# Down-projection of a transformer block: sums added to the rows by two accumulating DMAs, and a fifteenth Strassen pair in the second half

## The chip, the cores and the metric

One NeuronCore of a Trainium2 chip runs the whole program. The metric is the device time of one execution in microseconds (us). The core has a matrix engine (PE in the profile, with PEld for its weight loads), a vector engine (DVE), a scalar engine (ACT), GpSimd (POOL), a queue engine that issues transfers (SP), and 16 DMA engines that all queues share. Each engine runs its own list of instructions strictly in order, and waits on semaphores of the others.

## The reference

One decoder layer on 256 tokens of width 2048 in float32. The part that matters here is the end of it:

```python
D_FF = ((8 * D_MODEL // 3 + 255) // 256) * 256        # 5632

def conv_glu_ffn(h, w_up, cw, cb, w_down):
    u = causal_depthwise_conv(h @ w_up, cw, cb)
    a, gate = jnp.split(u, 2, axis=-1)
    return (jax.nn.silu(gate) * a) @ w_down
...
    x = x + jnp.concatenate([attn, conv], axis=-1) @ w_out[l]
    h = rms_norm(x, ffn_norm_g[l])
    x = x + conv_glu_ffn(h, w_up[l], ffn_conv_w[l], ffn_conv_b[l], w_down[l])
return rms_norm(x, final_norm_g)
```

The down-projection multiplies the gated rows g (256 x 5632) by w_down (5632 x 2048) and adds the product to the rows x, which are then normed and written out.

## The kernel before, in words

**Halves and pairs.** The down-projection runs in two halves of 1024 output columns (`for h in range(2)`). Each half takes 22 pairs of 128-row slices of w_down. Below the pairs are counted through both halves: 0 to 21 are the first half, 22 to 43 the second. A half holds eight PSUM banks (`nb`): four of them (names 2, 3, 4, 8) collect the four 128 x 512 quarters of the output, the other four (1, 5, 6, 7) collect corrections that Strassen pairs need. The two halves use the eight banks in turned roles (`ring`), so a bank of the second half is free when what the first half left in it has been read.

**Two kinds of pair.** `KINDS` has a letter for each pair. A direct pair (D) is eight products of a 128-row slice. A Strassen pair (S) is seven products, in the order of `products`; the third and fourth use sums of gated slices (`gs`, part 1), the fifth and sixth use sums of gated slices (`gs`, part 0) and sums of weights (`xh`, `xl`). Every product is four matmuls in split precision: a float32 operand is held as a high part and a low part (`wh` and `wl` for weights, `gh` and `gl` for gated slices), so each weight chunk costs ACT one copy (`wh`) and DVE one subtraction (`wl`), line 113 and 114. A Strassen chunk costs more: DVE makes three sums of weights (lines 139 and 142, tile `sums`, one buffer), and ACT and DVE split these into `xh` and `xl`. Tiles `xh` and `xl` share a ring of four buffers (`tag="xt"`), so two Strassen chunks are under way at a time. The subtraction that gives `xl` is written at the start of the next chunk's split (`lows`).

**Order of the work.** The program is written out by hand; nothing reorders it. `down_pair` runs up to four entries of a list `todo` (five before pair 21), then `w_next` splits the chunk two pairs ahead, then the pair's matmuls are issued. Splitting a chunk also lets SP issue the transfer of the chunk four ahead (`w_dma`).

**POOL's queue.** During the down-projection POOL only issues transfers: `gl` (512 KB, the low parts of four gated slices, at every second pair, line 1083) and `gs` (two of 256 KB for each Strassen pair, two pairs ahead, line 1090). Earlier, in the up-projection, POOL also writes the third weight sum of each Strassen chunk into DRAM with one plain and two accumulating transfers of 256 KB (line 1108), and forms the sums of gated slices for all pairs that are S in either half (`SPAIRS`, lines 1099 to 1101).

**Between the halves.** When the last Strassen pair of a half (pair 20) has been issued, `combine` is put on `todo`: ACT copies bank 1 to `cuv`, and eight DVE additions put the corrections into the rows `x2`. `cuv` has the buffer of `sums`, so the next Strassen split waits for it. At pair 22 four `first_add` (DVE: rows plus the four main banks) and four `first_half` (ACT: squares for the final norm; DVE: product with the final gain) follow.

Of the kernel before, what the change touches and what calls it, by code (L numbers as in the profile page):

```python
# [11 lines left out]
F32 = mybir.dt.float32  # L12
F32R = mybir.dt.float32r
AF = mybir.ActivationFunctionType
OP = mybir.AluOpType
PSUM = bass.MemoryType.PSUM

P = 128
# [16 lines left out]
CW = 2048  # L35
# [1 line left out]

SLOT = {(0, 0): 0, (1, 1): 1, (1, 0): 2, (0, 1): 3}
KINDS = ("DDDDSSDSSSSDSSSSDSSSSD",
         "DDSDSSDSSSDSSSSDSSSSDD")  # L40
SPAIRS = [p for p in range(22) if "S" in KINDS[0][p] + KINDS[1][p]]

CUTS = ((0, 1), (1, 2), (2, 4), (4, 5), (5, 6), (6, 8), (8, 10), (10, 12), (12, 14), (14, 16))
# [10 lines left out]
def hybrid_trunk(ctx: ExitStack, tc: tile.TileContext, a: dict, out: bass.AP):  # L54
    nc = tc.nc
# [123 lines left out]
    def w_next(cuts=1, ahead=LA):  # L179
        c = st["use"]  # L180
        st["use"] += 1
        w_pump()
        if st["split"] >= len(chunks):
            for f in lows:
                f()
            lows.clear()
        while st["split"] <= min(c + ahead, len(chunks) - 1):
            w_pump()
            w_split(cuts)
        if cuts == 1 or POOLED[0] <= st["split"] - 1 < POOLED[1]:  # L190
            w_pump()
        now = late[:]
        late.clear()
        if now:
            clock["dve"] = max(clock["dve"], clock["pe"])
        for f in now:
            f()
        return parts.pop(c)
# [54 lines left out]
    mixp = ctx.enter_context(tc.tile_pool(name="mix", bufs=1))  # L253
    xt = [mixp.tile([P, 4, 2, T], F32R, name="xt", bufs=4) for _ in range(4)]
# [3 lines left out]
    with ExitStack() as mx:  # L258
# [60 lines left out]
        for n, ((lo, hi), (xc, *wc)) in enumerate(zip(CUTS, heads)):  # L319
            xs = [(xc[:, (k - lo) * T:(k - lo + 1) * T], k) for k in range(lo, hi)]  # L320
            sl = slice(lo * P, hi * P)
            if n < EARLY:
                h, l = parts[0]
# [291 lines left out]
        for n in range(4):  # L615
            kv, i = divmod(n, 2)
# [360 lines left out]
        x2 = None  # L977
# [31 lines left out]
        for n, (qr, g) in enumerate(OUT_ORDER):  # L1009
# [3 lines left out]
            if n == 2:  # L1013
                x2 = mixp.tile([P, 2, D], F32, name="x2")
# [40 lines left out]
    with ExitStack() as fx:  # L1055
# [49 lines left out]
        for c in sorted(c for c in kinds if kinds[c] == "S"):  # L1105
            src, far = chunks[c][0], spill.tile([P, 512], F32, name=f"sum{c - down0}")
# [109 lines left out]
        names = {(0, 0): 2, (0, 1): 3, (1, 0): 4, (1, 1): 8}  # L1216
# [9 lines left out]
        def run_todo(n):  # L1226
            for _ in range(min(n, len(todo))):
                todo.pop(0)()

        def down_pair(h, p, g, j, nb):  # L1230

            kind = KINDS[h][p]
            if j == 0 and h + p:
                g_load()
            run_todo(5 if 22 * h + p == 21 else 4)
            if not late_pool:
                ws = w_next()
                while stages:
                    up_stages()
                up_only.close()  # L1240
                late_pool.append(fx.enter_context(tc.tile_pool(name="fd", bufs=1)))
                sum_load(22 * h + p + 2, 1)
            else:
                sum_load(22 * h + p + 2, 1)
                ws = w_next()
            sum_load(22 * h + p + 2, 0)
            if kind == "S":
                gsum = sq.pop(0)
            for name, gi, w in products(kind, j):
                left[h, name] -= 1  # L1250
                wh, wl = [v[:, w % 4 * 512:(w % 4 + 1) * 512] for v in ws[w // 4 * 2:][:2]]
                xh, xl = [v[:, gi] for v in g] if gi < 8 else [gsum[gi // 2 % 2][:, i, gi % 2] for i in range(2)]
                mm_down(nb[name], xh, xl, wh, wl, (h, name) not in begun, left[h, name] == 0)
                begun.add((h, name))

        def combine(h, nb):

            x = {k: x2[:, k[0], h * 1024 + k[1] * 512:h * 1024 + (k[1] + 1) * 512] for k in names}
            s = {}

            def alloc():
                t = late_pool[0].tile([P, 1536], F32, name="cuv", tag="sums", bufs=1)
                s.update({n: t[:, i * 512:(i + 1) * 512] for i, n in enumerate("cuv")})
                nc.scalar.activation(s["c"], nb[1], AF.Copy)

            add, sub = nc.vector.tensor_add, nc.vector.tensor_sub
            return [alloc, lambda: add(x[0, 1], nb[5], x[0, 1]), lambda: add(x[1, 1], nb[5], x[1, 1]),
                    lambda: add(s["u"], nb[6], s["c"]), lambda: sub(s["v"], s["u"], nb[7]),
                    lambda: add(x[0, 0], x[0, 0], s["c"]), lambda: sub(x[0, 1], x[0, 1], s["u"]),
                    lambda: add(x[1, 0], x[1, 0], s["v"]), lambda: sub(x[1, 1], x[1, 1], s["v"])]  # L1270

        def first_add(nb, t, n):
            xq = x2[:, t, n * 512:(n + 1) * 512]
            nc.vector.tensor_add(xq, nb[names[t, n]], xq)

        def first_half(t, n):
            xq = x2[:, t, n * 512:(n + 1) * 512]
            nc.scalar.activation(sq3[:, :512], xq, AF.Square, accum_out=ss3[:, t, n:n + 1])
            nc.vector.tensor_mul(xq, xq, gfin[:, n * 512:(n + 1) * 512])
# [3 lines left out]
        def last_rows(w0, w1_, g, b0, t):  # L1283
            for i, (lo, hi) in enumerate(LAST):
                b = (b0, bank[2 + t], bank[4 + t])[i][:, :hi - lo]
                for j, ws in enumerate((w0, w1_)):
                    for k in range(2):
                        n = lo // 512
                        c = slice(SLOT[k, n] * 512 + lo - n * 512, SLOT[k, n] * 512 + hi - n * 512)
                        gs = 4 * j + 2 * k + 1 - t  # L1290
                        mm_down(b, g[0][:, gs], g[1][:, gs], ws[0][:, c], ws[1][:, c],
                                i > 0 and j + k == 0, j + k == 2)
                xq = x2[:, t, 1024 + lo:1024 + hi]
                if i == 2:
                    acc = mean_of(fw, [ss3[:, t, i:i + 1] for i in range(3)], D)
                nc.vector.tensor_add(xq, b, xq)
                nc.scalar.activation(sq3[:, :hi - lo], xq, AF.Square, accum_out=ss3[:, t, 2 + i:3 + i])
            r3 = rstd_of(fw, [ss3[:, t, i:i + 1] for i in range(3, 5)], D, acc)
            xq = x2[:, t].rearrange("p (a b c) -> p a b c", a=2, b=2)
            for i in range(2):  # L1300
                nc.scalar.activation(xq[:, 0, i], xq[:, 0, i], AF.Copy, scale=r3)
                nc.vector.scalar_tensor_tensor(xq[:, 1, i], xq[:, 1, i], r3, gfin[:, 1024 + i * 512:1536 + i * 512],
                                               op0=OP.mult, op1=OP.mult)
                nc.sync.dma_start(out_rows[:, t].rearrange("p (a b c) -> p a b c", a=2, b=2)[:, :, i], xq[:, :, i])

        begun, todo, left = set(), [], {}
# [5 lines left out]
                for name in (2, 4):  # L1312
                    left[h, name] += 1
        ring = bank[2:] + bank[:2]
        prev = None
        for h in range(2):
            nb = dict(zip((2, 3, 4, 8, 1, 5, 6, 7), ring[4 * h:] + ring[:4 * h]))
            for q in range(NQ):
                g = gq.pop(0)
                if h == 1 and q == NQ - 1:  # L1320
                    run_todo(99)
                    for t in range(2):
                        nc.vector.tensor_add(x2[:, t, 1536:], nb[names[t, 1]], x2[:, t, 1536:])
                    w0 = w_next()
                    w1_ = w_next()
                    for t in range(2):
                        last_rows(w0, w1_, g, nb[names[t, 0]], t)
                    break
                if prev and q == 0:
                    todo.extend(lambda t=t, n=n, nb=prev: first_add(nb, t, n) for t in range(2) for n in range(2))  # L1330
                    todo.extend(lambda i=i: first_half(i // 2, i % 2) for i in range(4))
                for j in range(2):
                    p = 2 * q + j
                    down_pair(h, p, g, j, nb)
                    if KINDS[h].rfind("S") == p:
                        todo.extend(combine(h, nb))
            prev = nb


def _buckets():  # L1340
# [87 lines left out]
```

## Time and profile before

| what | value |
|---|---|
| median of 3 runs | 1086.2 us (1086.03 to 1087.13) |
| the profiled execution, its time | 1086.44 us |
| its span on the core | 1084.7 us |
| up-projection on PE | to 849.2 us |
| down-projection on PE | 849.2 to 1075.2 us |
| granted PE clock | 1.00 in all stretches read here |

Times of rows are counted from the start of the span. The span is 1.74 us shorter than the execution. In an answer on stretches of time, each engine's busy time is followed by its number of instructions, then come the granted PE clock, the mean busy share of the 16 DMA engines and what they moved in GB/s. In a timeline row stand the start, the duration, the engine, the line, the operation, out<-in and the count; what the engine waited for just before is in brackets. A row on transfers has the size and the median time from issue to landing; a row on a queue (q0 is POOL's, q1 is SP's) has its packets, MB and share of the engines' time in that stretch.

### The profile page before, as it was taken

What the parts mean: (1) busy time and instruction counts of PE and PEld (TensorE: products, weight loads), DVE (VectorE), ACT (ScalarE), POOL (GpSimd) and SP (SyncE); (2) the same over time, 40 slices, a digit from 0 to 9 for tenths busy, and PEclk for the clock granted to TensorE, in tenths of its full rate; (3) what the DMA queues carried; (4) which work ended last, traced back from release to release, by engine and by line L of the source; (5) the groups of instructions that cost most, each with busy time, mean ns of one, the idle gap of its engine ahead of it and who ended that gap; (6) DMA issues with size and microseconds to landing.
All of it is one profiled execution on the core that took longest, in us unless ns stands there. A gap on an engine that the chain in (4) does not pass through costs nothing.

```text
span 1084.7 us, 17486 instructions
## 1 busy us (share of the span) xinstructions
PE 1073.1 (99%) x6730; PEld 956.5 (88%) x6730; DVE 878.1 (81%) x1399; ACT 615.7 (57%) x892; POOL 360.4 (33%) x411
## 2 busy tenths in 40 slices
PE   9999999999999999999999999999999999999996
PEld 9999999998788888888888888888888888888885
DVE  7899975777456677778787888878787899999996
ACT  7544366778635555556555555556555555655563
POOL 0888856657100202324233433212121222211220
PEclk9999999999999999999999999999999999999998
DMA  9676536323464788999999999966667699979882
GB/s 353 244 262 241 187 99 231 121 79 117 177 225 168 241 267 255 284 289 270 299 279 308 277 300 296 283 222 224 223 222 279 214 390 344 350 283 356 320 315 80
DMA packets 60048, 270.46 MB, mean 249 GB/s; under 512 B 7947, under 2 KB 10779, under 8 KB 39868
## 3 DMA queue, kind: packets, MB, share of 16 engines
q1 hardware_dynamic: 34156, 199.85, 51.2%
q0 software_dynamic: 22432, 62.93, 21.3%
q10 hardware_dynamic: 3376, 6.55, 1.7%
q8 instruction: 53, 0.87, 0.3%
q14 instruction: 31, 0.25, 0.1%
HBM read 252.51 MB, written 38.82 MB: 269 GB/s over the span
## 4 chain that ended last, share of the span: by engine, by line
PE 97%; DVE 2%; ACT 1%; issue 1%; DVEq 0%; POOLq 0%; POOL 0%; ACTq 0%
PE bank L1203 30%; PE bank L1205 15%; PE bank L212 6%; PE bank L210 6%; PE bank L201 5%; PE bank L203 5%; PE bank L202 5%; PE bank L213 3%; PE bank L211 3%; PE bank L218 3%; PE bank L220 3%; PE bank L219 3%; PE bank L923 1%; PE bank L900 1%; PE bank L855 1%
## 5 line engine op out<-in xcount | busy, mean ns | idle before, releaser
L1203 PE MATMUL bank<-xt,wh 128*128 128x512 f32 x1408 | 488.6, 394 | 0.0
L163 ACT ACTIVATE wh<-wraw 128x1024 fp32r<-128x1024 f32 (+2 forms) x193 | 270.0, 1418 | 288.0 <-PE bank L1203 113.4
L1205 PE MATMUL bank<-xt,wl 128*128 128x256 f32 x1408 | 390.1, 277 | 0.0
L168 DVE TENSOR_TENSOR wl<-wraw,wh 128x2048 fp32r<-128x2048 f32 (+1 forms) x139 | 260.4, 1879 | 106.1 <-ACT wh L163 105.4
L1203 PEld LDWEIGHTS bank<-xt,wh 128*128 128x128 f32 x1408 | 264.0, 188 | 61.1
L1205 PEld LDWEIGHTS bank<-xt,wl 128*128 128x128 f32 x1408 | 264.4, 188 | 0.0
L201 PE MATMUL bank<-xt,wh 128*128 128x256 f32 x502 | 143.8, 286 | 0.0
L203 PE MATMUL bank<-xt,wl 128*128 128x256 f32 x502 | 142.2, 283 | 0.8 <-DVE wl L168 0.8
L202 PE MATMUL bank<-xt,wh 128*128 128x256 f32 x502 | 142.0, 283 | 0.0
L168 POOL TENSOR_TENSOR wl<-wraw,wh 128x1024 fp32r<-128x1024 f32 (+1 forms) x54 | 121.1, 2273 | 30.8 <-ACT wh L163 30.8
L114 DVE TENSOR_TENSOR wl<-wraw,wh 128x2048 fp32r<-128x2048 f32 x44 | 100.3, 2284 | 4.6 <-ACT wh L113 4.5
L201 PEld LDWEIGHTS bank<-xt,wh 128*128 128x128 f32 x502 | 96.1, 191 | 1.5 <-issue 0.9
L203 PEld LDWEIGHTS bank<-xt,wl 128*128 128x128 f32 x502 | 96.1, 191 | 1.1 <-DVE wl L168 1.0
L202 PEld LDWEIGHTS bank<-xt,wh 128*128 128x128 f32 x502 | 96.2, 192 | 0.4
L468 DVE SCALAR_TENSOR_TENSOR bank<-us,cw,bank 128x256 f32<-128x256 f32 x232 | 93.7, 481 | 1.0 <-ACT bank L463 0.5
L1108 POOL DMA_DIRECT2D sum<-in_w_d x84 | 64.1, 833 | 81.2 <-issue 52.6
L113 ACT ACTIVATE wh<-wraw 128x2048 fp32r<-128x2048 f32 x44 | 83.0, 1903 | 7.8 <-PE bank L1203 4.0
L113 ACT ACTIVATE xh<-sums 128x1536 fp32r<-128x1536 f32 x28 | 41.8, 1491 | 78.1 <-DVE sums L142 58.6
L1142 DVE SCALAR_TENSOR_TENSOR yt<-u,fcw,yt 128x255 f32<-128x255 f32 (+1 forms) x176 | 80.9, 480 | 3.1
L1173 POOL DMA_DIRECT2D glf<-glt x22 | 12.9, 585 | 183.0 <-DVE glt L114 131.5
L210 PE MATMUL bank<-wh,gh 128*128 128x512 f32 x167 | 65.6, 393 | 0.0
L891 POOL TENSOR_SCALAR e<-e,lsum 128x128 f32<-128x128 f32 x64 | 55.6, 886 | 29.9 <-ACT qs L778 17.0
(263 smaller groups left out, 1839.3 us busy)
## 6 DMA issues: line engine op xcount, KB each, us to landing
wraw<-in_w_u SPq DMA_DIRECT2D x88, 1024.0 KB, 7.7
wraw<-in_w_t SPq DMA_DIRECT2D x29, 1024.0 KB, 5.1
sum<-in_w_d POOLq DMA_DIRECT2D x84, 256.0 KB, 8.7
wraw<-in_w_d SPq DMA_DIRECT2D x28, 768.0 KB, 7.0
wraw<-in_w_o SPq DMA_DIRECT2D x16, 1024.0 KB, 4.9
wraw<-in_w_d SPq DMA_DIRECT2D x16, 1024.0 KB, 7.5
gs<-gsf POOLq DMA_DIRECT2D x56, 256.0 KB, 6.6
gl<-glf POOLq DMA_DIRECT2D x22, 512.0 KB, 5.6
```

The lines of the kernel that those rows point to most:

```text
L113: nc.scalar.activation(hi, src, AF.Copy)
L114: return lambda: nc.vector.tensor_sub(lo, src, hi.bitcast(F32))
L163: nc.scalar.activation(h[:, sl], raw[:, sl], AF.Copy)
L168: (nc.gpsimd if pooled else nc.vector).tensor_sub(l[:, sl], raw[:, sl], h[:, sl].bitcast(F32))
L201: nc.tensor.matmul(ps, wh, xh, start=first, stop=False)
L202: nc.tensor.matmul(ps, wh, xl, start=False, stop=False)
L203: nc.tensor.matmul(ps, wl, xh, start=False, stop=last)
L210: nc.tensor.matmul(ps, xh, wh, start=first, stop=False)
L468: nc.vector.scalar_tensor_tensor(y[:, j] if last else acc[0], us[:, j, k:k + T], cw[:, j, k:k + 1], acc[0], op0=OP.mult, op1=OP.add)
L1142: nc.vector.scalar_tensor_tensor(ys[i][:, d:], us_[i][:, :T - d], fcw[:, c, k:k + 1], ys[i][:, d:], op0=OP.mult, op1=OP.add)
L1203: nc.tensor.matmul(bk[i], wh[:, k, sl], xt[kt // 4][:, kt % 4].rearrange("p a t -> p (a t)"), start=kt == 0, stop=False)
L1205: nc.tensor.matmul(bk[i][:, :T], wl[:, k, sl], xt_h[kt], start=False, stop=kt == KD - 1)
```

## The change

1. Pair 25 becomes a Strassen pair: `KINDS[1]` has S in place 3, so the second half has fifteen. Pair 3 thereby joins `SPAIRS`: in the up-projection its gated sums are formed, split and stored, and the third weight sum of chunk 25 is built by three more transfers.
2. Between the halves, `combine_far` takes the place of `combine` and `first_add`. ACT copies bank 1 to a tile v in the `xt` ring, four DVE operations make all four corrections in v, and POOL adds v to the rows with one accumulating transfer of 1 MB (`near`). ACT then copies the four main banks to a second tile v (`take`), which a second accumulating transfer adds to the same rows.
3. `first_half` moves from pair 22 to pairs 28 to 31, one quarter ahead of each.

```diff
-         "DDSDSSDSSSDSSSSDSSSSDD")
+         "DDSSSSDSSSDSSSSDSSSSDD")
...
-        def first_add(nb, t, n):
-            xq = x2[:, t, n * 512:(n + 1) * 512]
-            nc.vector.tensor_add(xq, nb[names[t, n]], xq)
+        def combine_far(nb):
+
+            v = []
+
+            def far():
+                v.append(mixp.tile([P, CW], F32R, name="xh", tag="xt", bufs=4).bitcast(F32)
+                         .rearrange("p (t n c) -> p t n c", t=2, n=2))
+                return v[-1]
+
+            def near():
+                nc.gpsimd.dma_start(x2[:, :, :1024], v[-1].rearrange("p t n c -> p t (n c)"), accum_op=OP.add)
+
+            def take(t, n):
+                nc.scalar.activation(v[-1][:, t, n], nb[names[t, n]], AF.Copy)
+
+            add, sub = nc.vector.tensor_add, nc.vector.tensor_sub
+            return [lambda: nc.scalar.activation(far()[:, 0, 0], nb[1], AF.Copy),
+                    lambda: add(v[0][:, 0, 1], nb[6], v[0][:, 0, 0]), lambda: sub(v[0][:, 1, 0], v[0][:, 0, 1], nb[7]),
+                    lambda: sub(v[0][:, 0, 1], nb[5], v[0][:, 0, 1]), lambda: sub(v[0][:, 1, 1], nb[5], v[0][:, 1, 0]),
+                    near, lambda: (far(), take(0, 0), take(0, 1)), lambda: take(1, 0), lambda: take(1, 1), near]
...
-                if prev and q == 0:
-                    todo.extend(lambda t=t, n=n, nb=prev: first_add(nb, t, n) for t in range(2) for n in range(2))
-                    todo.extend(lambda i=i: first_half(i // 2, i % 2) for i in range(4))
+                if h and q == 3:
+                    for i in range(4):
+                        todo.extend([lambda: None] * 3 + [lambda i=i: first_half(i // 2, i % 2)])
...
-                        todo.extend(combine(h, nb))
+                        todo.extend(combine(h, nb) if h else combine_far(nb))
```

**POOL's order, before**, from the `gl` load that is issued at pair 22 (`gs1` and `gs0` are parts 1 and 0; `gsf0` is pair 24's, `gsf1` here pair 26's, `gsf2` pair 27's; names in brackets are semaphores waited for, DMASW those of POOL's own transfers):

```order
L1083 DMA gl_9726<-glf1_4159 128x1024 [waits DMASW4_49,DMASW0_49,PE_49]
L1090 DMA gs1_9732<-gsf0_4169 128x512
L1090 DMA gs0_9747<-gsf0_4169 128x512 [waits DMASW7_49,DMASW6_49]
L1083 DMA gl_9824<-glf2_4160 128x1024 [waits DMASW3_49,PE_49]
L1090 DMA gs1_9834<-gsf1_4170 128x512
L1090 DMA gs0_9849<-gsf1_4170 128x512 [waits DMASW2_49,DMASW1_49]
```

The same place after (now `gsf1` is pair 25's and `gsf2` pair 26's; `x2` are the rows, `xh_9701` and `xh_9745` the two tiles v):

```order
L1083 DMA gl_9742<-glf1_4159 128x1024 [waits DMASW5_49,DMASW1_49,PE_49]
L1282 DMA x2_3578<-xh_9701 128x2x1024 [waits DMAHW5_49,DVE_49,Activation_49]
L1090 DMA gs1_9750<-gsf0_4169 128x512 [waits DMASW3_49]
L1090 DMA gs0_9765<-gsf0_4169 128x512 [waits DMASW4_49]
L1282 DMA x2_3578<-xh_9745 128x2x1024 [waits DMASW2_49,Activation_49]
L1090 DMA gs1_9800<-gsf1_4170 128x512 [waits DMASW6_49]
L1090 DMA gs0_9815<-gsf1_4170 128x512 [waits DMASW7_49]
L1083 DMA gl_9849<-glf2_4160 128x1024 [waits DMASW0_49,PE_49]
L1090 DMA gs1_9851<-gsf2_4171 128x512 [waits DMASW1_49]
```

The two accumulating transfers stand ahead of the `gs` loads of pairs 24 and 25. DMASW2, for which the second one waits, is the semaphore that the first one raises when it has landed.

**DVE's order, before**, from the subtraction for chunk 24:

```order
L114 TENSOR_TENSOR wl_9735<-wraw_9622,wh_9734 128x2048 [waits Activation_49]
L1274 TENSOR_TENSOR x2_3578<-bank2_66,x2_3578 128x512 [waits PE_49]
L1274 TENSOR_TENSOR x2_3578<-bank3_67,x2_3578 128x512 [waits PE_49]
L1274 TENSOR_TENSOR x2_3578<-bank4_68,x2_3578 128x512 [waits PE_49]
L1274 TENSOR_TENSOR x2_3578<-bank5_69,x2_3578 128x512 [waits PE_49]
L114 TENSOR_TENSOR xl_9737<-sums_9738,xh_9736 128x1536 [waits Activation_49]
L114 TENSOR_TENSOR wl_9787<-wraw_9659,wh_9786 128x2048 [waits DMAHW1_49,Activation_49]
L1279 TENSOR_TENSOR x2_3578<-x2_3578,gfin_4154 128x512 [waits Activation_49] x4
L139 TENSOR_TENSOR sums_9840<-wraw_9695 128x1024 [waits DMAHW3_49,DMAHW2_49,DVE_49]
```

And after, from the same instruction to the subtraction for chunk 26:

```order
L114 TENSOR_TENSOR wl_9753<-wraw_9637,wh_9752 128x2048 [waits Activation_49]
L114 TENSOR_TENSOR xl_9755<-sums_9756,xh_9754 128x1536 [waits PE_49,Activation_49]
L139 TENSOR_TENSOR sums_9807<-wraw_9674 128x1024 [waits DMAHW2_49,DMAHW1_49,DVE_49]
L142 TENSOR_TENSOR sums_9807<-wraw_9674 128x512
L114 TENSOR_TENSOR wl_9804<-wraw_9674,wh_9803 128x2048 [waits PE_49,Activation_49]
L114 TENSOR_TENSOR xl_9806<-sums_9807,xh_9805 128x1536 [waits DMASW5_49,Activation_49]
L139 TENSOR_TENSOR sums_9858<-wraw_9711 128x1024 [waits DMAHW4_49,DMAHW3_49,DVE_49]
L142 TENSOR_TENSOR sums_9858<-wraw_9711 128x512
L114 TENSOR_TENSOR wl_9855<-wraw_9711,wh_9854 128x2048 [waits Activation_49]
```

The four additions and four products are gone from here, and chunk 25 has sums and an `xl` of its own. That `xl_9806` takes the buffer of the second v and so waits for DMASW5, which the second accumulating transfer raises when it has landed. On ACT, `xh` of chunk 25 takes the buffer of the first v and waits for the first transfer likewise.

More of the change, by code (lines that the diff above doesn't have):

```diff
@@ L1314, in hybrid_trunk @@
         ring = bank[2:] + bank[:2]
-        prev = None
         for h in range(2):
@@ L1335, in hybrid_trunk @@
                     if KINDS[h].rfind("S") == p:
-                        todo.extend(combine(h, nb))
-            prev = nb
+                        todo.extend(combine(h, nb) if h else combine_far(nb))
 def _buckets():
```

## The prediction

> **What bounds the kernel now.** I read the page's busy times first, then the chain that ended last, then stretches of the down-projection, then the timelines of PE, DVE and POOL around the boundary of the halves.
>
> ```profile
> PE 1073.1 (99%) x6730; PEld 956.5 (88%) x6730; DVE 878.1 (81%) x1399; ACT 615.7 (57%) x892; POOL 360.4 (33%) x411
> PE 97%; DVE 2%; ACT 1%; issue 1%; DVEq 0%; POOLq 0%; POOL 0%; ACTq 0%
> 400.00:450.00 50.00, 50.00 (x290) 43.74 (x290) 38.87 (x54) 27.69 (x36) 12.16 (x17) 1.00 0.85 254
> 960.00:980.00 20.00, 20.00 (x115) 17.46 (x114) 19.97 (x22) 10.22 (x13) 4.36 (x8) 1.00 0.76 268
> 980.00:1060.00 80.00, 80.00 (x460) 70.06 (x459) 78.48 (x53) 47.72 (x29) 16.29 (x30) 1.00 0.88 319
> ```
>
> PE is busy without a gap, and the chain is PE's own work. So time is saved only by giving PE less to do, and any wait put on PE is lost in full. In the down-projection DVE is nearly full too (78.48 of 80), so it can't catch up quickly after a delay. What room it has is read from its distance to PE. These are PE's first matmuls of pairs 24, 25, 26, 27 and 28, the first that needs `gs` in pair 24, and the second product of pair 25:
>
> ```profile
> 973.17 0.39 PE L210 MATMUL bank<-wh,gh 128*128 128x512 f32 x1
> 974.55 0.39 PE L210 MATMUL bank<-wh,gs 128*128 128x512 f32 x1
> 978.02 0.39 PE L210 MATMUL bank<-wh,gh 128*128 128x512 f32 x1
> 978.71 0.39 PE L210 MATMUL bank<-wh,gh 128*128 128x512 f32 x1
> 983.56 0.39 PE L210 MATMUL bank<-wh,gh 128*128 128x512 f32 x1
> 988.42 0.39 PE L210 MATMUL bank<-wh,gh 128*128 128x512 f32 x1
> 993.32 0.39 PE L210 MATMUL bank<-wh,gh 128*128 128x512 f32 x1
> ```
>
> A product takes 0.695 us (978.02 to 978.71 and on), a direct pair 5.55, a Strassen pair 4.87. Pair 25 is direct here.
>
> ```profile
> 955.94 1.29 DVE L1267 TENSOR_TENSOR x<-bank,x 128x512 f32<-128x512 f32 x2 [0.62 <-PE bank L220]
> 967.14 2.48 DVE L1274 TENSOR_TENSOR x<-bank,x 128x512 f32<-128x512 f32 x4
> 971.20 2.28 DVE L114 TENSOR_TENSOR wl<-wraw,wh 128x2048 fp32r<-128x2048 f32 x1
> 973.40 2.49 DVE L1279 TENSOR_TENSOR x<-x,gfin 128x512 f32<-128x512 f32 x4
> 979.75 1.75 DVE L114 TENSOR_TENSOR xl<-sums,xh 128x1536 fp32r<-128x1536 f32 x1
> 981.53 1.23 DVE L139 TENSOR_TENSOR sums<-wraw 128x1024 f32<-128x1024 f32 x1
> 983.28 2.28 DVE L114 TENSOR_TENSOR wl<-wraw,wh 128x2048 fp32r<-128x2048 f32 x1
> 985.48 1.75 DVE L114 TENSOR_TENSOR xl<-sums,xh 128x1536 fp32r<-128x1536 f32 x1
> ```
>
> By start times a Strassen chunk takes DVE 985.48 - 979.75 = 5.73 us (`xl` 1.75, two sums 1.75, `wl` 2.2), more than its pair takes PE; a direct one 2.2. A row addition is 0.62. Chunk 27's `wl` is ready at 985.5, and PE needs it in the third matmul of pair 27, at 988.42 + 0.35: DVE is 3.3 us ahead.
>
> **The change part by part.** *PE.* Pair 25 loses one product: -0.70 us, on the path.
>
> *Up-projection.* Pair 3's gated sums, their split, and five transfers more. PE has no gap in 400 to 450, where they fall, and DVE idles 11 us of 50 there: cost nothing, covered by PE's matmuls.
>
> *DVE.* Up to chunk 27, eight additions and four products go (12 x 0.62 = 7.4) and chunk 25's sums and `xl` come (3.5). Four products come back at pairs 28 to 31. DVE would be 3.9 us better off where the additions were; no gain, since PE wasn't waiting, but room.
>
> *ACT.* One copy stays, four come, the last of them after pair 21's end near 962. Behind them stands `wh` of chunk 24:
>
> ```profile
> 953.13 0.60 ACT L1264 ACTIVATE cuv<-bank 128x512 f32<-128x512 f32 x1 [0.90 <-DVE wl L114]
> L113 ACT ACTIVATE wh<-wraw 128x2048 fp32r<-128x2048 f32 x44 | 83.0, 1903 | 7.8 <-PE bank L1203 4.0
> ```
>
> It is ready near 962 + 0.6 + 1.9 = 964.5, so its `wl` is ready near 967, and PE needs both at 973: hidden. The four squares that move to pairs 28 to 31 lie in ACT's idle time (47.72 busy of 80), and SP's issues that a late `wl` holds back are for chunks four pairs on, some 20 us ahead.
>
> *The two transfers.* Here is POOL's queue at the boundary, and the last weight-sum addition in the up-projection:
>
> ```profile
> 962.58 0.55 POOL L1083 DMA_DIRECT2D gl<-glf  x1 [9.91 <-PE bank L220]
> 963.12 1.14 POOL L1090 DMA_DIRECT2D gs<-gsf  x2
> 684.83 0.92 POOL L1108 DMA_DIRECT2D sum<-in_w_d  x1 [4.14 <-issue]
> ```
>
> Both transfers stand behind that `gl`, which waits for PE's pair 21, so the first can't be issued before 963.1, though its four corrections are ready by some 958.4 (955.94 + 4 x 0.62). The second waits for the first's landing. Behind it in POOL's list stand pair 25's `gs` loads, the `gl` of pairs 26 and 27 and pair 26's `gs`; behind `xl` of chunk 25, which waits for the second landing, stand DVE's sums and `wl` of chunk 26. So all hangs on when they land. No row shows a 1 MB accumulating transfer within SBUF. The nearest, in order: that `gl`, a lone accumulating 256 KB (at 684.83), POOL's queue carrying plain bytes (966 to 968), and the same queue in two stretches of mostly accumulating bytes (686.4 to 688.6, 687.5 to 691.2):
>
> ```profile
> gl<-glf POOLq DMA_DIRECT2D x1, 512.0 KB, 6.5
> sum<-in_w_d POOLq DMA_DIRECT2D x1, 256.0 KB, 5.8
> q0 software_dynamic: 193, 0.70, 87.8%
> q1 hardware_dynamic: 25, 0.10, 12.0%
> q0 software_dynamic: 114, 0.23, 80.2%
> q0 software_dynamic: 133, 0.24, 36.4%
> ```
>
> Plain bytes move at 0.70 MB / (0.878 x 2 us) = 0.40 MB per us of all engines. Accumulating ones move at 0.24 / (0.364 x 3.7) = 0.178, or 0.23 / (0.802 x 2.2) = 0.130. So 1 MB (1.05 million bytes) takes the engines 5.9 to 8.1 us; I take 5.9, since in the slower stretch weight transfers share more of each engine's queue. The lone 256 KB landed in 5.8, of which 1.5 is bytes: 4.3 fixed, 10.2 for a whole transfer. The bounds: 5.8 if size costs nothing, 12.4 at the slower rate.
>
> First landing: `gl` lands at 962.58 + 6.5 = 969.1, and 5.9 more is 975.0; counted alone, 963.1 + 10.2 = 973.3. I take 974. Pair 24's `gs` follow 0.7 behind (256 KB at 0.40), 974.7 for a need at 974.55: no matter. Second landing, L: 974.1 + 10.2 = 984.3.
>
> Then, in steps from L. Pair 25's first `gs` lands at L + 0.7; PE needed it at 978.02 + 1.39 = 979.4. PE does five products and starts pair 26 at L + 4.2. DVE does `xl` of 25 and the sums and `wl` of 26 by L + 5.7, so pair 26's third matmul waits 1.15 us and the pair ends at L + 10.2. `wl` of 27 comes 5.73 later, L + 11.4; pair 27 waits another 0.85 and ends at L + 15.9. Before, pair 28 began at 993.32, so the loss is L - 977.4 = 6.9 us, the saved product included. From there DVE has no lead: each direct pair gives it 2.6 us, each Strassen pair after another takes 0.87, and each product at pairs 28 to 31 0.62. Followed through, pair 31 waits 0.4, pairs 35 and 36 1.2: 1.6 more. The tail after PE's last matmul stays as it is.
>
> Sum: 6.9 + 1.6 = 8.5 us. On the profiled execution's 1086.4 that is 1094.9; that execution is 0.24 above the median of the runs shown, so the forecast is 1086.2 + 8.5 = 1094.7.
>
> The row on sharing is weighed against a rule. In 966 to 968 POOL's queue had 87.8% of the engines and the weight queue 12.0%: the queues are served in bursts. The Trainium skill, "DMA: Bandwidth & Descriptors", section "SWDGE vs HWDGE vs iDMA", says that an engine takes turns between the queues of the two kinds. By it chunk 28's weights, issued near 967, would be dealt in between the first transfer's packets; this is the third rival, and the row here speaks rather against it.
>
> **The rivals.** *Hidden: not slower.* If size costs an accumulating transfer nothing beyond the lone 5.8 us, the first lands right behind `gl`, near 969.5, and L = 969.6 + 5.8 = 975.4. It decides at `wl` of chunk 27: L + 11.4 must be under 988.42 - 0.70 + 0.35 = 988.1, so L under 976.7. Then only the product counts: 1085.5. For it: 512 KB landed in 6.5, only 0.7 over the 256 KB. Against: the rates above.
> By the Trainium skill, same page, section "Anatomy of one DMA — SWDGE (gpsimd) path", a transfer of this kind takes 2.0 us and its bytes at 436 GB/s. An estimate from it: 4.4 us for 1 MB, L near 974, so it too gives 1085.5. The trace disagrees for accumulation: 256 KB would be 2.6 by it, and took 5.8.
>
> *DVE becomes the bound.* Fifteen Strassen chunks, transfers hidden. DVE's work in the second half changes by +3.5 - 7.4 + 2.5 = -1.4 us, so against; if the products at pairs 28 to 31 ate the lead, the 0.4 + 1.2 above would come, less 0.7: 1087.1.
>
> *Engines shared evenly.* 1 MB of chunk 28 at 0.40 MB per us puts 2.6 us on the first landing: L = 986.9, 1097.3.
>
> *Each transfer at the slower rate.* First 969.1 + 8.1 = 977.2, L = 977.3 + 12.4 = 989.7: 1100.1.
>
> **How the numbers follow.** Forecast 0.52, shared evenly 0.13, slower rate 0.10, hidden 0.19, DVE 0.04, anything else 0.02. The first three lie above 1088.4 and make slower 0.75; hidden and DVE make same 0.23; nothing read here could save 2.2 us, so faster has only the rest, 0.02. The bound of 2.2 us (0.2%) is about what can be told from no change. The range goes from the hidden case, 1085.4, to the slower rate, 1100.5; given that PE waits at all, 1089 to 1100.5.
>
> **What would show it.** A gap on PE in pair 25 before its first `gs` matmul, of L + 0.7 - 979.4, about 5.6 us; POOL's second accumulating issue waiting some 10 us for the first; DVE idle before `xl` of chunk 25 until the second landing; then short PE waits for `wl` at pairs 26 and 27. Wrong, if the two transfers land within 6 us each, or if the waits for `wl` vanish because DVE is quicker after its rest.

## The result, and the profile after

| | before | after |
|---|---|---|
| median of 5 runs each, side by side | 1086.3 us (1086.0 to 1087.1) | 1097.8 us (1097.6 to 1098.1) |
| ratio, with its 95% interval | | 1.0103 (1.0092 to 1.0115) |
| the profiled execution, its span | 1086.4, 1084.7 | 1098.1, 1096.3 |
| PE's last matmul starts | 1074.88 | 1085.48 |

The change makes the kernel 11.5 us slower; 8.5 was forecast. The page of the kernel after, its busy times and the shares of the chain that ended last:

```profile
PE 1075.7 (98%) x6726; PEld 956.6 (87%) x6726; DVE 877.4 (80%) x1395; ACT 619.2 (56%) x898; POOL 369.9 (34%) x423
PE 81%; DVE 8%; issue 5%; DMA 4%; ACT 1%; POOL 1%; SPq 0%; DVEq 0%; POOLq 0%; ACTq 0%
```

No engine's work has changed by more than a few us but POOL's, which has 9.5 more (360.4 before). But the chain, 97% PE before, now passes through transfers and DVE, which is read as: work that was beside PE has come onto its path. Where, POOL's timeline of the kernel after shows, from the `gl` load of pair 22 on:

```profile
962.74 0.54 POOL L1083 DMA_DIRECT2D gl<-glf  x1 [9.91 <-PE bank L220]
963.50 1.25 POOL L1282 DMA_DIRECT2D x<-xh  x1 [0.22 <-issue]
964.25 1.67 POOL L1090 DMA_DIRECT2D gs<-gsf  x2
975.19 1.26 POOL L1282 DMA_DIRECT2D x<-xh  x1 [9.28 <-DMA x<-xh]
975.92 1.67 POOL L1090 DMA_DIRECT2D gs<-gsf  x2
978.06 0.54 POOL L1083 DMA_DIRECT2D gl<-glf  x1 [0.47 <-issue]
986.04 1.08 POOL L1090 DMA_DIRECT2D gs<-gsf  x2 [7.44 <-issue]
```

The second accumulating transfer is issued at 975.19, after 9.28 us of waiting for the first; the two `gs` loads of pair 25 come only behind it. The next two rows are the accumulating transfers' own, in the chain of waits (start, duration to landing), and then what PE and DVE waited for in their timelines:

```profile
963.50 10.97 DMA x<-xh
975.19 10.54 DMA x<-xh
```

```profile
976.64 0.50 PE L210 MATMUL bank<-wh,gs 128*128 128x512 f32 x1 [1.77 <-DMA gs<-gsf]
986.40 0.50 PE L210 MATMUL bank<-wh,gs 128*128 128x512 f32 x1 [3.03 <-DMA gs<-gsf]
970.54 2.28 DVE L114 TENSOR_TENSOR wl<-wraw,wh 128x2048 fp32r<-128x2048 f32 x1
985.83 1.76 DVE L114 TENSOR_TENSOR xl<-sums,xh 128x1536 fp32r<-128x1536 f32 x1 [13.01 <-DMA x<-xh]
```

The first lands at 974.47, the second at 985.73. PE waits 1.77 us in pair 24 and 3.03 in pair 25, and DVE 13.01 before `xl` of chunk 25, since that takes the buffer of the second v. Between PE's two waits lies a stretch in which PE is busy but at half its granted clock (the 0.50 in the first row below). Behind them PE waits four times for `wl` (the second row: total, times, longest):

```profile
978.10:981.40 3.30, 3.30 (x13) 2.82 (x12) 0.00 (x0) 0.00 (x0) 0.50 (x1) 0.50 1.05 239
PE bank L212 <- DVE wl L114: 2.6, 4, 1.2
986.00:1075.00 89.00, 86.03 (x478) 73.82 (x479) 88.58 (x62) 52.98 (x39) 18.23 (x34) 1.00 0.81 291
```

The third row is the rest of the down-projection up to DVE's closing chain: DVE is busy for 88.58 of 89 us. Once it has lost 13 us it never idles again, and PE waits for it.

The DMA engines tell the same. These are the two queues in 960 to 1000, first of the kernel before, then of the one after (packets, MB, share of the engines' time; q0 is POOL's queue, q1 the weights'):

```profile
q1 hardware_dynamic: 1823, 7.74, 54.5%
q0 software_dynamic: 1289, 4.46, 29.9%
```

```profile
q0 software_dynamic: 1776, 6.29, 56.6%
q1 hardware_dynamic: 1269, 5.15, 33.5%
```

POOL's queue has nearly doubled its share of the engines for 1.83 MB more, and the weights have moved 2.6 MB less in the same 40 us. In the part in which the two transfers are under way, 963 to 986, the queues of the kernel after make 101.8%:

```profile
q0 software_dynamic: 1107, 4.06, 69.4%
q1 hardware_dynamic: 612, 2.91, 32.4%
```

Before, the same 23 us have 31.7 + 49.5 = 81.2%. A share adds up the times of packets, and these can overlap, so it can pass 100%; the engines are read as full there.

### The profile page after: what moved, and what is told of

Read it like the earlier page. It is cut to its first block, busy times and chain, and to the rows that moved or that the text cites. A ratio compares the mean times of both kernels' runs of the same rounds, so it can differ in the third digit from the quotient of the medians.

```text
span 1096.3 us, 17511 instructions
## 1 busy us (share of the span) xinstructions
PE 1075.7 (98%) x6726; PEld 956.6 (87%) x6726; DVE 877.4 (80%) x1395; ACT 619.2 (56%) x898; POOL 369.9 (34%) x423
## 4 chain that ended last, share of the span: by engine, by line
PE 81%; DVE 8%; issue 5%; DMA 4%; ACT 1%; POOL 1%; SPq 0%; DVEq 0%; POOLq 0%; ACTq 0%
PE bank L1203 30%; PE bank L1205 15%; PE bank L201 5%; PE bank L203 5%; PE bank L202 5%; DVE wl L114 3%; PE bank L218 3%; PE bank L220 3%; PE bank L219 3%; PE bank L212 2%; PE bank L210 2%; DVE xl L114 2%; DMA x<-xh 2%; DMA wraw<-in_w_t 1%; PE bank L213 1%
## 5 line engine op out<-in xcount | busy, mean ns | idle before, releaser
L1108 POOL DMA_DIRECT2D sum<-in_w_d x87 | 66.7, 854 | 71.5 <-issue 50.9
L212 PE MATMUL bank<-wl,gh 128*128 128x512 f32 x161 | 63.8, 396 | 2.6 <-DVE wl L114 2.6
L891 POOL TENSOR_SCALAR e<-e,lsum 128x128 f32<-128x128 f32 x64 | 55.6, 885 | 29.9 <-ACT qs L778 17.0
```

The costliest lines, as they stand in the source:

```text
L212: nc.tensor.matmul(ps, xh, wl, start=False, stop=False)
```

## The experiments

Before the first of them my theory was "landings": the loss comes from where the two transfers land, since loads and buffers that PE and DVE need stand behind them. Rival A was the load that the fifteenth Strassen chunk puts on DVE, rival B the extra traffic itself, slowing every transfer wherever the two stand. Times are medians, with the ratio to the kernel before on the same chip (1086.6 to 1086.7 there) and its 95% interval.

**1. Pair 25 direct again**, in the kernel after.

```diff
-         "DDSSSSDSSSDSSSSDSSSSDD")
+         "DDSDSSDSSSDSSSSDSSSSDD")
```

> The changed kernel with pair 25 direct again: both accumulating transfers stay. Theory (landings): the loss hangs on what stands behind the second landing, near 985.7. With pair 25 direct, pair 26 is the first to need what stands behind it (its gl near 987, its xl near 987.3), and PE gets there at 983.6 plus the 1.9 us wait and the slower stretch of pair 24: 1088 to 1090.5. Rival A (the fifteenth Strassen chunk is too much for DVE): 1086. Rival B (the extra traffic slows all transfers): near 1097.

1095.15 us, 1.0080 (1.0066 to 1.0094). A miss for the number: 4.6 us above the range of theory "landings", 2 us under rival B's. Without the pair nothing in pair 25 needs `gs`, but PE then waited 3.6 us for the `gl` load of pair 26, which stands behind the second transfer too. So most of the loss is the transfers' and not the fifteenth pair's, but taking away one late load only brings the next.

**2. Pair 25 as a Strassen pair alone**, in the kernel before.

```diff
-         "DDSDSSDSSSDSSSSDSSSSDD")
+         "DDSSSSDSSSDSSSSDSSSSDD")
```

> The kernel before with pair 25 as a Strassen pair and nothing else. Theory (landings): no transfer to wait for; the product saves 0.7 us, and chunk 25's 3.5 us on DVE use up the 3.3 us by which DVE led, so short waits for wl at pair 27, about 0.9: 1086.5, within 0.2% of before. Rival A: most of the 11.5 us, 1094 or more. Rival B: 1085.6 to 1086.5.

1087.85 us, 1.0013 (1.0004 to 1.0022). What PE waited for in the down-projection, and the engines in 980 to 1060:

```profile
PE bank L212 <- DVE wl L114: 1.2, 2, 0.7
980.00:1060.00 80.00, 78.77 (x450) 68.51 (x449) 79.69 (x55) 48.05 (x29) 16.85 (x31) 1.00 0.88 322
```

DVE is full (79.69 of 80, 78.48 before), and PE pays for the product that it saves with 1.2 us of waits. Rival A is worth some 1.2 us alone, not 11: it is out as the cause.

**3. The first transfer ahead of `gl`**, so that it doesn't stand behind pair 21.

```diff
+            run_todo(5 if 22 * h + p == 21 else 4)
             if j == 0 and h + p:
                 g_load()
-            run_todo(5 if 22 * h + p == 21 else 4)
```

> The changed kernel with the first accumulating transfer issued ahead of the gl load of pair 22, so that it doesn't wait for PE's pair 21 (about 958.6 in place of 963.5). Theory (landings): both landings come about 5 to 6 us earlier, the second near 980, and the time falls by as much, to 1091.5 to 1092.5; pair 24's wait for gs goes too. Rival A: no change, 1097.8. Rival B: no change, since the bytes are the same, 1097 to 1098.

1096.28 us, 1.0088 (1.0074 to 1.0102): a miss. The first was issued at 958.90, 4.6 us sooner, the second at 971.79, 3.4 sooner. But the second took 12.4 us to land instead of 10.5, the `gs` loads of pair 25 landed at 985.3 and 985.9 behind it, and PE waited 3.8 us for them.

**4. The `gs` loads of pair 25 ahead of the second transfer.**

```diff
+            if 22 * h + p == 23:
+                sum_load(25, 1)
+                sum_load(25, 0)
             run_todo(5 if 22 * h + p == 21 else 4)
...
```

> The changed kernel with pair 25's two gs loads issued ahead of the second accumulating transfer. PE then has its operands, but DVE's xl of chunk 25 still waits for the second landing. Theory (landings), if DVE's chain from that landing on sets the end: no gain, 1097 to 1098.5, and PE's wait moves from the gs of pair 25 to its xl. If the gs wait set the time: 1094 or less. Rivals A and B: no change.

1099.12 us, 1.0135 (1.0101 to 1.0168; one of the four executions took 1108.5, the others 1098.1 to 1099.6), as expected no gain: PE's wait moved from `gs` to `xl` of chunk 25, which DVE can't make while the second v holds its buffer:

```profile
PE bank L212 <- DVE xl L114: 4.8, 1, 4.8
```

**5. The second v in a buffer of its own** (that of the final gain, which is loaded later; `first_half` comes one quarter later for that).

```diff
...
-                v.append(mixp.tile([P, CW], F32R, name="xh", tag="xt", bufs=4).bitcast(F32)
...
+                if v:
+                    t = fp.tile([P, D], F32, name="vfar", tag="gfin", bufs=1)
...
```

> The changed kernel with the second tile v in the buffer of the final gain (which is loaded later, by POOL at pair 28, and the four products at pairs 30 to 33), so that xl of chunk 25 waits for the first landing only; pair 25's gs loads still stand behind the second transfer. Theory (landings): PE waits for gs until about 986.4 as before, but DVE isn't held, so the waits for wl at pairs 26 and 27 and later go: pair 26 starts near 989.9 in place of 983.56, and the time is 1092 to 1093.5. Rival A: no change or slower, 1097.8. Rival B: no change.

1096.80 us, 1.0094 (1.0079 to 1.0110): a miss. DVE's wait for the transfers fell from 13.0 to 4.0 us, but PE still waited 5.5 for `gs`, in two waits.

**6. Four and five together** (both diffs as above).

> Both of it: gs of pair 25 ahead of the second transfer, and the second tile v in a buffer of its own. Theory (landings): pair 25 doesn't wait, but the gl of pairs 26 and 27 is still queued behind the second transfer, landing near 988.3, and PE wants it near 985 to 987 (after pair 24's wait): 1090 to 1091.5. Rival A: 1097.8. Rival B: no change, since every byte is moved as before, at nearly the same time.

1092.69 us, 1.0059 (1.0045 to 1.0072), 1.2 over the upper end expected and 5 under rival B's "no change". Together they gain 5.1 us, where alone they gained 1.0 and lost 1.3: the late `gs` and the held buffer end at the same landing, and either alone leaves the other.

**7. Three, four and five together** (all three diffs).

> As the last, with the first transfer also ahead of the gl load of pair 22. The same two transfers, the same bytes, fifteen pairs. Theory (landings): second landing near 980, gl of pairs 26 and 27 near 982, before PE wants it at 983: no wait is left, and only the saved product counts, 1085.3 to 1086.5. Rival A: 1095 or more. Rival B: 1095 or more.

1094.72 us, 1.0075 (1.0062 to 1.0087): the worst miss, and no better than the sixth. POOL's timeline of this kernel shows what the theory had left out:

```profile
958.72 1.26 POOL L1293 DMA_DIRECT2D x<-xh  x1 [5.59 <-DVE xh L1301]
970.22 1.08 POOL L1093 DMA_DIRECT2D gs<-gsf  x2 [5.51 <-issue]
975.68 1.25 POOL L1293 DMA_DIRECT2D x<-vfar  x1 [4.38 <-issue]
985.28 1.09 POOL L1093 DMA_DIRECT2D gs<-gsf  x2 [5.83 <-issue]
```

POOL stood still at the issue itself, three times for some 5 us, with no semaphore to wait for. Each time it went on 0.3 us after another transfer had landed: the first at 969.9, pair 24's first `gs` at 975.4, the second at 985.0. The kernel after shows the same (7.44 at 986.04, the second landing at 985.73). Counted as 1 for a `gs` or `gl` load and 4 for an accumulating transfer, every such stop of the kernels after, 3 and 7 comes where an issue would make 8 under way at once, and none where it makes 7. The program sets aside 1024 bytes for the descriptors of POOL's transfers (an argument in `kernel`), so theory "room" was: that space is full. The Trainium skill, "DMA: Bandwidth & Descriptors", section "SWDGE vs HWDGE vs iDMA", says that POOL writes the descriptors of its transfers into rings in SBUF, from which the DMA engines take them; no run here shows the rings themselves.

**8. Plain copies**: the two transfers replace the rows instead of adding to them, so the sum over the halves is left out.

```diff
-                nc.gpsimd.dma_start(x2[:, :, :1024], v[-1].rearrange("p t n c -> p t (n c)"), accum_op=OP.add)
+                nc.gpsimd.dma_start(x2[:, :, :1024], v[-1].rearrange("p t n c -> p t (n c)"))
```

> The changed kernel with the two transfers as plain copies onto the rows, without the addition (the rows are then not the sums). Same size, same order, same waits. Theory (landings): a plain 1 MB takes the engines 2.6 us where an accumulating one took 5.3, so the second landing comes 5 to 6 us earlier: 1091.5 to 1093. Rival A: 1097.8. Rival B: half the added traffic, so about half the loss, 1092.

1094.20 us (1090.79 to 1095.51), 1.0064 (1.0047 to 1.0081): 3.6 us under the kernel after, 1.2 over the upper end expected; rival B had 1092, so this run does not tell the two theories apart by its time. The profiled execution is the quickest of the four, 1090.79. Its rows on what PE waited for, on the two transfers, and on the queues in 960 to 1000:

```profile
PE bank L212 <- DVE wl L114: 1.7, 3, 0.6
x<-xh POOLq DMA_DIRECT2D x2, 1024.0 KB, 7.0
q0 software_dynamic: 1870, 6.66, 47.3%
q1 hardware_dynamic: 1619, 7.03, 46.4%
```

The same 1 MB landed in 7.0 us instead of 10.8, PE waited for no transfer, and POOL never stopped at an issue for over 0.3 us. In the packet records of 955 to 995, 4096 bytes of POOL's queue take about 161 ns when copied; in the kernel after a second group of 470 packets lies between 310 and 340 ns, where the kernel before has 6. So adding costs twice the engines' time: 512 packets x 0.33 us / 16 = 10.6 us of all engines for both transfers, 5.2 for copies. The kernel before leaves 100 - 54.5 - 29.9 = 15.6% of those 40 us free, 6.2 us.

That gave two theories for the last four kernels: "room", and what their texts call rival "traffic" (rival B: the price is the engines' time, wherever the transfers stand), beside DVE's own waits.

**9. The room doubled**, in the kernel after (the square's unused output moves to other tiles to make space).

```diff
-    nc = _bacc.Bacc("TRN2", target_bir_lowering=False, num_devices=1, dynamic_dma_scratch_size=1024)
+    nc = _bacc.Bacc("TRN2", target_bir_lowering=False, num_devices=1, dynamic_dma_scratch_size=2048)
...
```

> The kernel after with the room for the descriptors of POOL's transfers doubled (1024 to 2048 bytes; the square's waste output lies in two constants that are no longer used, to make space for it). Theory 'room': only so many of POOL's transfers can be under way, counted as 1 for a gs or gl load and 4 for an accumulating transfer, with 7 in all; the next issue waits until one has landed. With 15 in all POOL's 7.44 us at 986.04, put down to issue, falls under 1 us. But the second transfer still waits for the first to land and the gs loads of pair 25 still land behind it, so TensorE keeps about 3 us in pair 25 and DVE its 13 us: 1096.5 to 1098. Rival: the wait at issue has nothing to do with the room, and 5 us or more of it stay; the time is the same then, so the wait tells the two apart, not the time.

1098.04 us, 1.0105 (1.0091 to 1.0119). POOL's timeline from the second transfer on:

```profile
976.71 1.24 POOL L1282 DMA_DIRECT2D x<-xh  x1 [11.46 <-DMA x<-xh]
977.44 1.64 POOL L1090 DMA_DIRECT2D gs<-gsf  x2
978.54 1.07 POOL L1083 DMA_DIRECT2D gl<-glf  x1
979.06 1.08 POOL L1090 DMA_DIRECT2D gs<-gsf  x1
```

The 7.44 us stop is gone, as theory "room" says, and so is every other over 0.3. The time is that of the kernel after: there the stop lasted until 0.3 us behind the second landing, and the loads that it held back stood behind that transfer in the queue anyway.

**10. The room doubled, in the seventh kernel** (the diff of 9 on the three).

> The kernel with all three moves (first transfer ahead of gl, gs loads of pair 25 ahead of the second transfer, second tile in a buffer of its own), 1094.7, with the room doubled and nothing else changed. Theory 'room': POOL's 5.5 and 4.4 us at issue go; the second transfer is issued when the first has landed, at about 970.3 instead of 975.7, lands about 981.5, the gl of pair 26 behind it at about 984 where it is needed at 984.3, TensorE's waits of 3.1 and 0.95 us go, and with them most of the slow stretch behind them: 1086.5 to 1089. Rival 'DVE': the end is set by DVE's own waits (3.2 for ACT at 965, 3.9 for ACT's xh, 4.5 for ACT's square at 1012), which the room does not touch: 1092 to 1095.

1095.68 us, 1.0081 (1.0068 to 1.0093): a miss for "room". POOL's second issue, the two transfers' times to landing, and PE's wait in pair 26:

```profile
971.24 1.24 POOL L1293 DMA_DIRECT2D x<-vfar  x1 [5.97 <-DMA x<-xh]
x<-xh POOLq DMA_DIRECT2D x1, 1024.0 KB, 11.7
x<-vfar POOLq DMA_DIRECT2D x1, 1024.0 KB, 15.1
989.11 0.58 PE L211 MATMUL bank<-wh,gl 128*128 128x256 f32 x1 [4.45 <-DMA gl<-glf]
```

The stops went and the second transfer was issued 4.4 us sooner than in the seventh kernel, as said. It only took longer, 15.1 us against 9.3, and landed later than there, at 986.4 against 985.0; `gl` came behind it. So the stop at the issue is real, but was not what the time hung on.

**11. The room doubled, and DVE's product with the gains a pair behind ACT's square**, in the seventh kernel.

```diff
-                    for i in range(4):
-                        todo.extend([lambda: None] * 3 + [lambda i=i: first_half(i // 2, i % 2)])
+                    for i in range(5):
+                        todo.extend([lambda i=i: first_gain((i - 1) // 2, (i - 1) % 2) if i else None] + [lambda: None] * 2
+                                    + [lambda i=i: first_half(i // 2, i % 2) if i < 4 else None])
```

> The kernel before this one, and DVE's product with the gains one pair after ACT's square of the same piece, so that DVE doesn't stand behind ACT there. Theory 'room': nearly all is gained by the room already, and this adds 0 to 1 us: 1086 to 1088.5. Rival 'DVE': 3 to 4.5 us faster than the kernel with the room alone.

1094.18 us, 1.0064 (1.0050 to 1.0078). 1.5 us under the tenth in the medians, their ranges overlapping (1092.6 to 1095.6 against 1094.0 to 1096.4): the 3 to 4.5 of rival "DVE" is not there. The wait of 4.4 us that was taken away came back as longer waits of `xl` for ACT's `xh` (6.0 to 9.6 us).

**12. The second transfer behind the loads of pair 26**, with the room doubled and gains apart, the first transfer ahead of `gl` and the second v in a buffer of its own, as in the eleventh; pair 25's `gs` loads stand at their usual place.

```diff
             sum_load(22 * h + p + 2, 0)
+            if 22 * h + p == 24:
+                second[0]()
...
```

> The room doubled, gains apart, first transfer ahead of gl, second tile in a buffer of its own, and the second transfer one pair later: behind gl and the gs loads of pair 26, so that nothing that pairs 25 and 26 need is queued behind it. Theory 'room' (with the place of the loads): second transfer issued about 976.5, lands about 987.5; the gs loads of pair 27 behind it land about 989 to 990 and are needed at about 990.5; no wait over 0.5 us on TensorE but the three of 0.6 for wl that the fifteenth pair makes: 1086 to 1088.5. Rival 'traffic': a transfer of this size costs TensorE some us wherever it stands, because the weights' loads share the engines with it: 1090 or more.

1093.02 us, 1.0059 (1.0046 to 1.0071): a miss for "room with the place of the loads", and what rival "traffic" expected. PE's one wait for a transfer, its half clock behind it, and the queues in 960 to 1000:

```profile
993.59 0.79 PE L210 MATMUL bank<-wh,gs 128*128 128x512 f32 x1 [4.39 <-DMA gs<-gsf]
993.00:999.40 6.40, 5.81 (x18) 4.94 (x19) 5.87 (x5) 1.35 (x1) 0.06 (x1) 0.50 1.02 422
q0 software_dynamic: 1842, 6.86, 57.0%
q1 hardware_dynamic: 1664, 7.01, 45.2%
```

Nothing that pairs 25 and 26 need stands behind the second transfer now, and PE runs through both. But that transfer took 13.2 us, so pair 27's `gs` landed at 993.5 instead of 989 to 990. 57.0 and 45.2 are 102% of the engines: they are full. In the seventh and tenth kernel the two queues make 102.7 and 102.9%. The half clock costs PE nearly as much as the wait: it held from 992.83 to 999.66, 6.07 us of it behind the wait, which is some 3.0 us of work lost. 4.39 + 3.0 - 0.7 for the saved product is 6.7, and PE's last matmul is 6.73 us later than before (1081.61 against 1074.88). That is the profiled execution, 1094.3; two others, 1092.0 and 1092.2, kept a granted clock of 0.997 over the span, as the kernel before does, so the half clock is not in all of them.

**What follows.** Seven kernels with the transfers at other places, with other buffers and more room (3, 5 to 7, 10 to 12) took 1092.7 to 1096.8 us. Place and buffers matter: the sixth moves the same bytes and is 5.1 us quicker than the kernel after, so rival B's "wherever the two stand" is refuted. But some 6 us stay in the best of the seven. Most took away the wait that they aimed at, and in each another load came late, in 40 us in which 10.6 us of work are put into 6.2 us of free engine time. The 102%, and the eighth kernel, in which the packets take half the time, a transfer lands in 7.0 us and PE waits for none, show that the engines' time sets how late the transfers land.

Not shown is that this is the whole of the 6 us. By the same sum the 5.2 us of the copies fit into the free 6.2, and the eighth kernel still lost 4.1 us in its profiled execution and 7.5 in the median. The sum is rough: it leaves out the two `gs` loads and the third weight sum that pair 25 adds itself. The eighth kernel's other executions, 1093.1 to 1095.5, were not profiled; their granted clock over the whole span is 0.993 to 0.995, against 0.997 in the profiled one and before, so half-clock stretches are likely there too. Not tried: less traffic with the sum kept. No kernel here beats the one before.

## Why the prediction came out right, point by point

The mechanism was the one forecast, and each sign that was named is there: PE's gap in pair 25 (3.03 us where some 5.6 was forecast, since PE came there late), POOL's 9.28 us for the first, DVE idle until the second landing, short waits for `wl` at pairs 26 (1.22) and 27 (0.53). The sum was 3.1 us short of the span's 11.6. The misses of its terms all go the same way, so none hid another.

*First landing:* 974 forecast, 974.47 measured. Right, with a little luck: 974 was taken between two counts, 973.3 and 975.0, and the transfer was issued 0.4 us later and took 0.8 longer than the first of them has.

*Pair 24's `gs`, "no matter":* failed. They landed from 976.6 on, not at 974.7. The queues in 966 to 968 and in 971 to 975 of the kernel after:

```profile
q0 software_dynamic: 149, 0.54, 102.6%
q1 hardware_dynamic: 2, 0.01, 0.8%
q1 hardware_dynamic: 115, 0.94, 59.4%
q0 software_dynamic: 128, 0.43, 42.3%
```

First POOL's queue has the engines alone, then chunk 28's weights take more than half while the first transfer's last packets and `gs` are moved. It cost PE 1.77 us and some 1.65 by the half clock; neither is added to the sum, since PE would have stood in pair 25 instead: it came there at 986.40 - 3.03 = 983.4, not 979.4. That this step did no harm to the forecast is luck. The second pair of rows agrees with the rule of the Trainium skill that the engines take turns ("DMA: Bandwidth & Descriptors", "SWDGE vs HWDGE vs iDMA"). The stretch ahead of it does not: chunk 28's weights were issued at 967.12, their first packet moved at 971.20, and in 967 to 971 POOL's queue alone had 108.1%. What held them back isn't shown.

```profile
967.12 0.33 SPq L106 DMA_DIRECT2D wraw<-in_w_d  x1
q0 software_dynamic: 215, 0.86, 108.1%
```

The rival of engines shared evenly, 1097.3, is near the measured time but not by its own steps: it has the first landing 2.6 us later, which did not happen.

*Second landing, L:* 984.3 forecast, 985.73 measured: issued at 975.19 instead of 974.1, and 10.54 instead of 10.2 on its way. Mis-sized by 1.4. The engines' time that it counts for a transfer was near, 5.9 us against the 5.3 of the packet records. The estimate from the Trainium skill's fit ("DMA: Bandwidth & Descriptors", "Anatomy of one DMA — SWDGE (gpsimd) path"), 4.4 us, is out: 10.5 and 11.0 here, 7.0 for copies.

*From L to pair 28:* L + 15.9 would be 1001.63; pair 28 starts here:

```profile
1002.10 0.39 PE L210 MATMUL bank<-wh,gh 128*128 128x512 f32 x1
```

0.5 more. *Later waits:* 1.6 forecast; PE's last matmul is 10.60 late and pair 28 was 8.78, so 1.8.

*"The tail after PE's last matmul stays as it is":* failed. These are DVE's first additions of the closing chain, before and after:

```profile
1063.22 1.29 DVE L1267 TENSOR_TENSOR x<-bank,x 128x512 f32<-128x512 f32 x2 [0.74 <-PE bank L220]
1075.41 1.28 DVE L1267 TENSOR_TENSOR x<-bank,x 128x512 f32<-128x512 f32 x2
```

Before, DVE waited there for PE; after, it waits for nothing and is itself late, by 12.2 us where PE is by 10.6. The span grew by 11.6, 1.0 more than PE's delay. 1.4 + 0.5 + 0.2 + 1.0 = 3.1.

*The saved product, -0.70:* counted as gained, but the second experiment shows that DVE eats it: alone the pair costs 1.2 us. The rival "DVE becomes the bound" had 0.9 for that.

## What to carry to other kernels

A transfer that takes work off an engine must be paid in the DMA engines' time: add up its packets and compare with what the two queues leave free in that stretch, before looking for a better place in the order. A sum that doesn't fit is a warning; one that fits is no promise, as the eighth kernel shows. Ask of every load queued behind it, and of every buffer it holds, when the next reader comes; where two of them end at the same landing, taking one away shows nothing. And where a second engine is nearly as full as the bound (78.5 of 80 us here), its idle time during the wait is lost for good, and the end must be followed through it too.

## What the runs showed of the hardware that was not expected

- An accumulating packet of 4096 bytes within SBUF takes 310 to 340 ns, a plain one 161.
- With 1024 bytes for descriptors POOL stops at an issue when more than 7 units would be under way (256 KB and 512 KB loads 1, a 1 MB accumulating transfer 4), and goes on 0.3 us after a landing. With 2048 bytes no such stop was left.
- The same accumulating 1 MB took 9.0 to 15.8 us from issue to landing (experiments 5 and 11).
- A wait of PE can be followed by a stretch at granted clock 0.50: 3.4 us of it (978.1 to 981.5) behind a wait of 1.77 in the kernel after, 6.8 with one of 4.39 in the twelfth, only 3.4 with one of 4.82 in the fourth, and none behind one of 3.03 in the kernel after. The Trainium skill, "TensorE: Matmul & The Clock Gate", "Part 1: The HAM clock gate (the "warmup" mystery)", has half the clock after an idle window of about 3.4 us that runs freely; the lengths, one and two windows, agree with it, the wait of 1.77 is shorter than the page's figure.
